# Loading and reducing the last tile of a sum-of-absolute-values kernel in three pieces, with a vector-engine transpose and early stores for the output

## The chip, the cores and the metric

The kernel runs on one core of one Trainium2 chip. The metric is the device time of one execution in microseconds (us), lower is better. The time before is 50.15 us (median of 6 runs, 50.07 to 50.20). The profile covers a span of 48.4 us of this; the remaining 1.75 us lie outside the span and nothing here touches them.

The engines that matter are VectorE (DVE in the profile), ScalarE (ACT), TensorE (PE), and SyncE (SP), which issues most DMAs.

## The reference

```python
batch, dim = 1024, 4096
x = np.random.randn(batch, dim).astype(np.float32)
def reference(x, axis):            # axis = -1
    return np.sum(np.abs(x), axis=axis).astype(np.float32)
```

The input is 16.78 MB and the output 4 KB.

## The kernel before

The 1024 rows are eight tiles of 128 rows. Each tile has a buffer of its own, so no load ever waits for compute. Vector reduces the left 2048 columns of a tile, ACT the right 2048. The ending adds the two halves, transposes the [128 rows, 8 tiles] result on PE so that the store has long rows, copies it out of PSUM (the memory that PE wrote it to) and stores it with one DMA of 8 rows of 512 B.

```python
for t in range(n_tiles):                       # 8
    x_tile = xpool.tile([P, dim], x.dtype)
    nc.sync.dma_start(out=x_tile[:], in_=x[bass.ts(t, P)])
    nc.vector.tensor_reduce(out=vres[:, t : t + 1], in_=x_tile[:, 0:v_cols],
                            axis=X, op=add, apply_absolute_value=True)
    nc.scalar.activation(out=act_scratch[:], in_=x_tile[:, v_cols:dim],
                         func=Abs, accum_out=sres[:, t : t + 1])
res = small.tile([P, n_tiles], fp32)
nc.vector.tensor_add(out=res[:], in0=vres[:], in1=sres[:])
psum_t = psum_pool.tile([P, P], fp32)
nc.tensor.transpose(out=psum_t[0:n_tiles, :], in_=res[:], identity=ident[:])
out_sb = small.tile([n_tiles, P], fp32)
nc.vector.tensor_copy(out=out_sb[:], in_=psum_t[0:n_tiles, :])
nc.sync.dma_start(out=out_tp, in_=out_sb[:])
```

(Enum names are shortened here. Line 53 is the load, 55 the vector reduce, 71 the add, 74 the transpose, 77 the copy, 79 the store.)

## Time and profile before

| what | number | view |
|---|---|---|
| one 2 MB tile arrives every | 4.89 us | timeline: starts of consecutive vector reduces |
| vector reduce of 2048 columns | 2.29 us | groups of instructions |
| ACT on 2048 columns | 1.88 us + 0.19 us accumulator read | groups of instructions |
| last tile landed to end of span | 5.5 us | chain of waits |

First, the rows of the page that cut the span into 40 equal slices: busy tenths of an engine, then the same for the DMA engines, then what they moved.

```profile
DVE  0000000890089007910791069106920692059420
ACT  3600000880078007900690069005900591059100
DMA  0969999999999999999999999999999999300000
GB/s 0 190 217 406 433 433 420 433 433 433 433 433 433 433 433 433 433 433 420 433 433 433 433 433 420 420 420 420 433 433 406 433 433 433 163 0 0 0 3 0
```

The DMA engines are full from slice 4 to slice 34, near 433 GB/s. Vector and ACT are idle more than half the time. So the load stream is the limit, and shortening compute in the middle is worth nothing. The last five slices, about 6 us, have no load in them: there the compute is exposed.

The groups of instructions give the busy time and the mean of one instruction, then the idle time before them and what ended it:

```profile
L55 DVE TENSOR_REDUCE vres<-x_tile 128x1 f32<-128x2048 f32 x8 | 18.3, 2286 | 26.9 <-DMA x_tile<-in_x_dram 26.9
L63 ACT ACTIVATE act_scratch<-x_tile 128x2048 f32<-128x2048 f32 x8 | 15.0, 1881 | 26.9 <-DMA x_tile<-in_x_dram 26.9
```

All idle time of both is waiting for a load. Last, the end of the chain of waits (start in us, duration in us, what):

```profile
4.43 38.41 DMA x_tile<-in_x_dram
42.85 0.02 issue
42.87 2.30 DVE vres L55
...
45.27 0.18 DVE res L71
45.45 0.14 issue
45.58 0.39 PE psum_t L74
45.97 0.02 issue
45.99 0.28 DVE out_sb L77
```

After the last landing at 42.87 come 2.3 us for a whole half tile, 1.1 us from there to the store's issue at 46.30, and 2.1 us from issue to the end at 48.4.

### The profile page before, as it was taken

To read this page: it belongs to the slowest core of one execution; us is meant where nothing else is said; L and a number is where in the kernel's file an instruction comes from. 1 tells how busy PE (TensorE), PEld (TensorE's weight loads), DVE (VectorE), ACT (ScalarE), POOL (GpSimd) and SP (SyncE) were. 2 spreads that over 40 slices of the span, in tenths; PEclk is the share of its full clock that TensorE was granted. 3 is DMA by queue.
4 is the path that set the end of the run, shared out by engine and by line. 5 is a ranking of instruction groups with operands and counts; after the bars stand their busy time and mean duration, and the time that the engine had idled before them with its cause. 6 is when DMAs were issued, how large, how long until landed. Compare 5 with 4: busy or idle time off the path is not lost.

```text
span 48.4 us, 99 instructions
## 1 busy us (share of the span) xinstructions
PE 0.4 (1%) x1; PEld 0.1 (0%) x1; DVE 18.7 (39%) x10; ACT 17.3 (36%) x17; POOL 0.7 (1%) x6
## 2 busy tenths in 40 slices
PE   0000000000000000000000000000000000000300
PEld 0000000000000000000000000000000000000000
DVE  0000000890089007910791069106920692059420
ACT  3600000880078007900690069005900591059100
POOL 5000000000000000000000000000000000000000
DMA  0969999999999999999999999999999999300000
GB/s 0 190 217 406 433 433 420 433 433 433 433 433 433 433 433 433 433 433 420 433 433 433 433 433 420 420 420 420 433 433 406 433 433 433 163 0 0 0 3 0
DMA packets 1168, 16.78 MB, mean 347 GB/s; under 512 B 136, under 2 KB 144, under 8 KB 144
## 3 DMA queue, kind: packets, MB, share of 16 engines
q1 hardware_dynamic: 1168, 16.78, 82.9%
HBM read 16.78 MB, written 0.00 MB: 347 GB/s over the span
## 4 chain that ended last, share of the span: by engine, by line
DMA 79%; SPq 7%; DVE 6%; issue 1%; PE 1%; DVEq 0%
DMA x_tile<-in_x_dram 79%; SPq L53 7%; DVE vres L55 5%; PE psum_t L74 1%; DVE out_sb L77 1%; DVE res L71 0%; DVEq L71 0%
## 5 line engine op out<-in xcount | busy, mean ns | idle before, releaser
L55 DVE TENSOR_REDUCE vres<-x_tile 128x1 f32<-128x2048 f32 x8 | 18.3, 2286 | 26.9 <-DMA x_tile<-in_x_dram 26.9
L63 ACT ACTIVATE act_scratch<-x_tile 128x2048 f32<-128x2048 f32 x8 | 15.0, 1881 | 26.9 <-DMA x_tile<-in_x_dram 26.9
L63 ACT ACT_TABLE_LOAD x1 | 1.3, 1283 | 0.7 <-PEq L96 0.7
L63 ACT ACTIVATION_READ_ACCUMULATOR act_scratch<-x_tile 128x1 f32 x8 | 1.5, 186 | 0.0
L74 PE MATMUL psum_t<-ident,res 128*8 128x128 f32 x1 | 0.4, 372 | 45.6 <-DVE res L71 45.6
L77 DVE COPY out_sb<-psum_t 8x128 f32<-8x128 f32 x1 | 0.3, 279 | 0.6 <-PE psum_t L74 0.6
masks.py:199 POOL TENSOR_SCALAR_AFFINE_SELECT ident<-ident 128x128 f32<-128x128 f32 x1 | 0.3, 292 | 0.1
masks.py:197 POOL MEMSET ident<- 128x128 f32 x1 | 0.2, 205 | 0.3 <-POOLq L96 0.3
L71 DVE TENSOR_TENSOR res<-vres,sres 128x8 f32<-128x8 f32 x1 | 0.2, 166 | 0.1
L74 PEld LDWEIGHTS psum_t<-ident,res 128*8 128x8 f32 x1 | 0.1, 84 | 45.5 <-issue 45.5
L96 POOL MEMSET const-float32-0.0<- 128x1 f32 x1 | 0.1, 98 | 0.2 <-issue 0.2
L96 POOL MEMSET const-bfloat16-1.0<- 128x1 bf16 x1 | 0.1, 101 | 0.0
L96 POOL MEMSET const-uint8-127<- 128x1 uint8 x1 | 0.1, 101 | 0.0
L96 POOL MEMSET const-float32-1.0<- 128x1 f32 x1 | 0.1, 98 | 0.0
## 6 DMA issues: line engine op xcount, KB each, us to landing
x_tile<-in_x_dram SPq DMA_DIRECT2D x8, 2048.0 KB, 25.3
out_dram<-out_sb SPq DMA_DIRECT2D x1, 4.0 KB
```

The source lines that it names most:

```text
L53: nc.sync.dma_start(out=x_tile[:], in_=x[bass.ts(t, P)])
L55: nc.vector.tensor_reduce(out=vres[:, t : t + 1], in_=x_tile[:, 0:v_cols], axis=mybir.AxisListType.X, op=mybir.AluOpType.add, apply_absolu ...
L63: nc.scalar.activation(out=act_scratch[:], in_=x_tile[:, v_cols:dim], func=mybir.ActivationFunctionType.Abs, accum_out=sres[:, t : t + 1],)
L71: nc.vector.tensor_add(out=res[:], in0=vres[:], in1=sres[:])
L74: nc.tensor.transpose(out=psum_t[0:n_tiles, :], in_=res[:], identity=ident[:])
L77: nc.vector.tensor_copy(out=out_sb[:], in_=psum_t[0:n_tiles, :])
L96: nc = _bacc.Bacc("TRN2", target_bir_lowering=False, num_devices=1)
```

## The change

It shortens what lies behind the last landing. It loads the last tile in three DMAs of 2432, 1216 and 448 columns and reduces each as it lands; it finishes and stores the results of the first seven tiles (rows 0 to 6 of the output, seen as 8 rows of 128) while the last one is still loading; and it replaces add, PE transpose and PSUM copy by one small reduce and a vector transpose of 32x32 blocks. Since blocks are transposed in place, the last tile's results (row 7 of the output) for its rows 0 to 31 land in one partition, for rows 32 to 63 in another 32 partitions on, and so forth. By writing the result into columns 0 and 31 of the pad (a tile of 32 columns of zeros that the transpose reads), two of the four land in adjacent partitions (31, 32 and 95, 96), so two stores of two rows suffice, one on SP and one on ACT.

```diff
+LAST_TILE_PIECES = [      # share of columns, share of these to vector
+    (0.59375, 0.50),       # 2432 columns: vector 1216, ACT 1216
+    (0.296875, 0.345),     # 1216 columns: vector 416, ACT 800
+    (0.109375, 1.00),      #  448 columns: vector 448
+]
 ... loads of tiles 0 to 6 as before ...
+    for s, e, _ in pieces:
+        nc.sync.dma_start(out=x_last[:, s:e], in_=last_rows[:, s:e])
 ... reduces of tiles 0 to 6 as before ...
+    nc.vector.tensor_add(out=res06_pad[:, 0:n_full], in0=p06_v[...], in1=p06_s[...])
+    nc.vector.transpose(out=t06[:], in_=res06_pad[:])
+    for b in range(n_blk):                                   # 4 early stores
+        nc.sync.dma_start(out=out_tp[0:n_full, b * BS : (b + 1) * BS],
+                          in_=t06[b * BS : b * BS + n_full, 0:BS])
+    for s, e, ve in pieces:
+        ... vector reduce of [s:ve] and ACT of [ve:e], each into its column of p7 ...
-    nc.vector.tensor_add(out=res[:], in0=vres[:], in1=sres[:])
-    nc.tensor.transpose(out=psum_t[0:n_tiles, :], in_=res[:], identity=ident[:])
-    nc.vector.tensor_copy(out=out_sb[:], in_=psum_t[0:n_tiles, :])
-    nc.sync.dma_start(out=out_tp, in_=out_sb[:])
+    nc.vector.tensor_reduce(out=res7_pad[:, 0:BS:BS - 1],
+        in_=p7[:, 0:n_parts].unsqueeze(1).to_broadcast([P, 2, n_parts]), axis=X, op=add)
+    nc.vector.transpose(out=res7T[:], in_=res7_pad[:])
+    nc.sync.dma_start(out=out7_dram[0:2], in_=res7T[BS - 1 : BS + 1, 0:BS])
+    nc.scalar.dma_start(out=out7_dram[2:4], in_=res7T[3 * BS - 1 : 3 * BS + 1, 0:BS])
```

(Cut and joined where marked; the memsets of the pads and the removal of the identity matrix are left out.)

More of the change, by code (lines that the diff above doesn't have):

```diff
@@ L7, with _round32 @@
 from concourse._compat import with_exitstack
-from concourse.masks import make_identity
-VECTOR_COLS_FRACTION = 0.5
-ACT_SCRATCH_SPACE = "psum"
+VECTOR_FRACTION = 0.5
+LAST_TILE_PIECES = [
[3 more added lines that the diff above has]
+]
+_VEC_NS_PER_COL, _VEC_FIXED = 1.042, 150.0
+_ACT_NS_PER_COL, _ACT_FIXED = 0.833, 480.0
+def _round32(v: int) -> int:
+    return (v // 32) * 32
 @with_exitstack
@@ L24 @@
     P = nc.NUM_PARTITIONS
+    fp32 = mybir.dt.float32
+    BS = nc.vector.STREAM_SQUARE_SIZE
     batch, dim = x.shape
@@ L28 @@
     n_tiles = batch // P
-    v_cols = int(dim * VECTOR_COLS_FRACTION) // 32 * 32
-    v_cols = max(32, min(v_cols, dim))
-    s_cols = dim - v_cols
+    n_full = n_tiles - 1
+    assert n_tiles <= BS, "output transpose layout assumes at most 32 row tiles"
+    assert dim % BS == 0, f"dim {dim} must be a multiple of {BS}"
+    assert P % BS == 0
+    n_blk = P // BS
+    v_cols = _round32(int(dim * VECTOR_FRACTION))
+    v_cols = min(max(v_cols, BS), dim)
+    pieces = []
+    pos = 0
+    for i, (frac, vshare) in enumerate(LAST_TILE_PIECES):
+        if i == len(LAST_TILE_PIECES) - 1:
+            end = dim
+        else:
+            end = min(dim, pos + max(BS, _round32(int(dim * frac))))
+        if end <= pos:
+            continue
+        vec_end = pos + _round32(int((end - pos) * vshare))
+        vec_end = min(max(vec_end, pos), end)
+        pieces.append((pos, end, vec_end))
+        pos = end
+        if pos >= dim:
+            break
+    n_parts = sum((1 if ve > s else 0) + (1 if e > ve else 0) for s, e, ve in pieces)
     out_tp = out.rearrange("(t p) -> t p", p=P)
@@ L38 @@
     psum_pool = ctx.enter_context(tc.tile_pool(name="psum", bufs=1, space=bass.MemoryType.PSUM))
-    ident = small.tile([P, P], mybir.dt.float32)
-    make_identity(nc, ident)
-    vres = small.tile([P, n_tiles], mybir.dt.float32)
-    sres = small.tile([P, n_tiles], mybir.dt.float32)
-    if ACT_SCRATCH_SPACE == "psum":
-        act_scratch = psum_pool.tile([P, s_cols], mybir.dt.float32)
-    else:
-        act_scratch = small.tile([P, s_cols], mybir.dt.float32)
-    for t in range(n_tiles):
-        x_tile = xpool.tile([P, dim], x.dtype)
-        nc.sync.dma_start(out=x_tile[:], in_=x[bass.ts(t, P)])
+    p06_v = small.tile([P, max(n_full, 1)], fp32)
+    p06_s = small.tile([P, max(n_full, 1)], fp32)
+    p7 = small.tile([P, max(n_parts, 1)], fp32)
+    res06_pad = small.tile([P, BS], fp32)
+    nc.gpsimd.memset(res06_pad[:], 0.0)
+    res7_pad = small.tile([P, BS], fp32)
+    nc.gpsimd.memset(res7_pad[:], 0.0)
+    s_max = max(
+        [dim - v_cols] + [max(e - ve, BS) for s, e, ve in pieces]
+    )
+    act_scratch = psum_pool.tile([P, s_max], fp32)
+    x_tiles = []
+    for t in range(n_full):
+        x_tile = xpool.tile([P, dim], x.dtype, name="x_tile")
+        nc.sync.dma_start(out=x_tile[:], in_=x[bass.ts(t, P)])
+        x_tiles.append(x_tile)
+    x_last = xpool.tile([P, dim], x.dtype, name="x_tile")
+    last_rows = x[bass.ts(n_full, P)]
+    for s, e, _ in pieces:
+        nc.sync.dma_start(out=x_last[:, s:e], in_=last_rows[:, s:e])
+    for t in range(n_full):
+        x_tile = x_tiles[t]
         nc.vector.tensor_reduce(
-            out=vres[:, t : t + 1],
+            out=p06_v[:, t : t + 1],
             in_=x_tile[:, 0:v_cols],
@@ L63 @@
         nc.scalar.activation(
-            out=act_scratch[:],
+            out=act_scratch[:, 0 : dim - v_cols],
             in_=x_tile[:, v_cols:dim],
             func=mybir.ActivationFunctionType.Abs,
-            accum_out=sres[:, t : t + 1],
+            accum_out=p06_s[:, t : t + 1],
         )
-    res = small.tile([P, n_tiles], mybir.dt.float32)
-    nc.vector.tensor_add(out=res[:], in0=vres[:], in1=sres[:])
-    psum_t = psum_pool.tile([P, P], mybir.dt.float32)
-    nc.tensor.transpose(out=psum_t[0:n_tiles, :], in_=res[:], identity=ident[:])
-    out_sb = small.tile([n_tiles, P], mybir.dt.float32)
-    nc.vector.tensor_copy(out=out_sb[:], in_=psum_t[0:n_tiles, :])
-    nc.sync.dma_start(out=out_tp, in_=out_sb[:])
+    if n_full > 0:
+        nc.vector.tensor_add(
+            out=res06_pad[:, 0:n_full], in0=p06_v[:, 0:n_full], in1=p06_s[:, 0:n_full]
+        )
+        t06 = small.tile([P, BS], fp32)
+        nc.vector.transpose(out=t06[:], in_=res06_pad[:])
+        for b in range(n_blk):
+            nc.sync.dma_start(
+                out=out_tp[0:n_full, b * BS : (b + 1) * BS],
+                in_=t06[b * BS : b * BS + n_full, 0:BS],
+            )
+    col = 0
+    for s, e, ve in pieces:
+        if ve > s:
+            nc.vector.tensor_reduce(
+                out=p7[:, col : col + 1],
+                in_=x_last[:, s:ve],
+                axis=mybir.AxisListType.X,
+                op=mybir.AluOpType.add,
+                apply_absolute_value=True,
+            )
+            col += 1
+        if e > ve:
+            nc.scalar.activation(
+                out=act_scratch[:, 0 : e - ve],
+                in_=x_last[:, ve:e],
+                func=mybir.ActivationFunctionType.Abs,
+                accum_out=p7[:, col : col + 1],
+            )
+            col += 1
+    nc.vector.tensor_reduce(
+        out=res7_pad[:, 0:BS:BS - 1],
+        in_=p7[:, 0:n_parts].unsqueeze(1).to_broadcast([P, 2, n_parts]),
+        axis=mybir.AxisListType.X,
+        op=mybir.AluOpType.add,
+    )
+    res7T = small.tile([P, BS], fp32)
+    nc.vector.transpose(out=res7T[:], in_=res7_pad[:])
+    out7_dram = out_tp[n_full].rearrange("(b j) -> b j", j=BS)
+    nc.sync.dma_start(out=out7_dram[0:2], in_=res7T[BS - 1 : BS + 1, 0:BS])
+    nc.scalar.dma_start(out=out7_dram[2:4], in_=res7T[3 * BS - 1 : 3 * BS + 1, 0:BS])
 _INS = ['x', 'axis']
```

## The prediction

> **What bounds the kernel now.** The load stream. The page shows the DMA engines at 90% or more and about 430 GB/s from 4 us to 41 us; in the timeline the vector reduces of consecutive 2 MB tiles start 4.89 us apart and last 2.29 us, so compute hides behind loading. Only the ends are exposed. The chain of waits after the last landing: vector reduce of 2048 columns 42.87 to 45.17, add 45.27 to 45.45, PE transpose 45.58 to 45.97, PSUM copy 45.99 to 46.27, output DMA issued 46.30 (0.35 us), end of span 48.4. That is 5.5 us after the last tile landed: 3.4 us of compute, 2.1 us from issue to end. The measured time is 1.75 us above the span.
>
> **What the change does.** It does not touch the 16.8 MB of loads. (1) The last tile comes in pieces of 2432, 1216 and 448 columns, so what must be computed after the last landing shrinks. (2) Rows 0 to 6 are added, transposed and stored before that. (3) Add, PE transpose and PSUM copy become one small vector reduce and one 32x32-block vector transpose; the last store is two 2-row DMAs, on SP and ACT.
>
> **Costs.** Fitting the trace, a vector reduce costs about 0.15 us + 1.04 ns per column (2.286 us at 2048), an ACT piece about 0.18 us + 0.83 ns per column plus a 0.19 us accumulator read. Scaling the 4.89 us per tile from tile 6's landing (37.99), the pieces land near 40.9, 42.35 and 42.9; smaller rows (9.7, 4.9, 1.8 KB instead of 16 KB) may cost 0.1 us more, so 43.0. Vector: 1216 columns to 42.35, 416 to about 43.0, 448 (0.62 us) to about 43.65. ACT: 1216 and 800 columns, finished near 43.4, not last. Rows 0 to 6's add and transpose fit at 40.3 to 40.8, in a hole. Final reduce (estimate 0.18 us, from the 0.17 us add) and transpose (estimate 0.2 us) end near 44.2. The last DMA issues near 44.25 instead of 46.30: 2.05 us earlier. About 1.55 us comes from the shorter last piece, 0.6 us from the shorter tail, less 0.1 us for loading.
>
> **Given back.** Store rows fall from 512 B to 128 B; the Trainium skill, "DMA: Bandwidth & Descriptors", Specifications, puts line rate at 512 B and up, with read-modify-write below. This trace does not show its latency. With six stores to wait for, and an ACT issue, I allow 0.1 us. The last issue to end should stay 2.1 to 2.4 us.
>
> **Predicted:** 48.2 us (span 46.4), 8 in 10 between 47.7 and 49.0. Faster by over 2%: 0.88; within 2%: 0.11; slower: 0.01.
>
> **What would show it right.** Vector's last big reduce has 448 columns, starts at 42.9 to 43.1, and lasts 0.6 us; the last DMA issues at 44.1 to 44.4; DMA slices up to 41 us unchanged; PE idle.
>
> **What would make it wrong.** The four early stores serialising on each other or getting in front of the last loads; false waits between vector and ACT, which write neighbouring columns of one partial-sums tile; SP stalling because ten loads and the stores reuse completion semaphores (the 9th DMA waited 3.7 us for the first load, harmlessly early); short stores with much longer completion; a last piece whose rows land late because one engine lags (in the trace the 16 engines' last packets end from 41.6 to 42.4 us).

## The result, and the profile after

The changed kernel takes 48.04 us (median of 8 runs, 47.94 to 48.09) against 50.09 us (16 runs). The ratio is 0.9585, 95% interval 0.9573 to 0.9598: faster. Ratios here are the mean time of one kernel's fast runs over that of the other's of the same rounds, so they are not quite the ratio of the medians quoted.

The same slices of the page after:

```profile
DVE  0000000594039601980089006930495019889810
ACT  3700000591029400960089005910393019558500
DMA  0959999999999998999999999999999899993000
```

The loads fill the same part of the span; behind them there are now three and a half slices instead of five and a half. A slice is 1.16 us here. The end of the chain of waits after:

```profile
8.58 33.81 DMA x_tile<-in_x_dram
42.40 0.02 issue
42.42 1.16 DVE p L130 x2
43.57 0.03 issue
43.60 0.05 DVEq L147
43.65 0.05 issue
43.70 0.18 DVE res_pad L147
43.88 0.02 issue
43.90 0.21 DVE res7T L154
```

The chain leaves the loads at 42.42, with the landing of the second piece. From there the view follows vector through the reduces of pieces two and three in one go, as there is no gap between them. That does not mean that the third piece was early. Each DMA raises a completion semaphore, a counter, when its data has landed. In the trace's records the third piece's semaphore got its last increment at 42.920, and the reduce of that piece started 0.022 us later, as the second piece's did (42.396 and 42.418). In all eight profiles that reduce these pieces as they land, the third reduce started 0.02 us after that increment:

```profile
42.42 0.59 DVE L130 TENSOR_REDUCE p<-x_tile 128x1 f32<-128x416 f32 x1
42.94 0.62 DVE L130 TENSOR_REDUCE p<-x_tile 128x1 f32<-128x448 f32 x1
```

The two reduces start 0.52 us apart; where all data had landed before (a run below), they start 0.49 us apart. So vector waited some 0.03 us for the third piece (0.02 to 0.06 us in the other seven): landing and compute end almost together, and the landing last. The timeline of the ending (start, duration, engine, line, operation) shows both engines:

```profile
40.39 0.17 DVE L116 TENSOR_TENSOR res_pad<-p_v,p_s 128x7 f32<-128x7 f32 x1
40.59 0.21 DVE L120 STREAM_TRANSPOSE t<-res_pad 128x32 f32<-128x32 f32 x1
40.83 1.38 SPq L122 DMA_DIRECT2D out_dram<-t  x4
40.90 2.67 DVE L130 TENSOR_REDUCE p<-x_tile 128x1 f32<-128x1216 f32 x3
...
42.48 0.84 ACT L139 ACTIVATE act_scratch<-x_tile 128x800 f32<-128x800 f32 x1 [0.21 <-DMA x_tile<-in_x_dram]
43.25 0.19 ACT L139 ACTIVATION_READ_ACCUMULATOR act_scratch<-x_tile 128x1 f32 x1
43.70 0.17 DVE L147 TENSOR_REDUCE res_pad<-p 128x2 f32<-128x10 f32 x1
43.90 0.21 DVE L154 STREAM_TRANSPOSE res7T<-res_pad 128x32 f32<-128x32 f32 x1
44.14 0.24 SPq L156 DMA_DIRECT2D out_dram<-res7T  x1
44.14 0.57 ACTq L157 DMA_DIRECT2D out_dram<-res7T  x1
```

Rows 0 to 6 are finished in the hole at 40.4 to 40.8, and their four stores are issued until 42.2 while the loads go on. From 40.9 to 43.6 both engines are nearly full; ACT is done at 43.44, vector at 43.56. The stores are issued at 44.14 instead of 46.30.

### The profile page after: what moved, and what is told of

It reads as the page before. It is cut to its first block, busy times and chain, and to the rows that moved or that the text cites. A ratio compares the mean times of both kernels' runs of the same rounds, so it can differ in the third digit from the quotient of the medians.

```text
span 46.3 us, 109 instructions
## 1 busy us (share of the span) xinstructions
DVE 19.3 (42%) x14; ACT 17.6 (38%) x19; POOL 0.4 (1%) x6
## 4 chain that ended last, share of the span: by engine, by line
DMA 90%; DVE 3%; issue 0%; DVEq 0%
DMA x_tile<-in_x_dram 90%; DVE p L130 2%; DVE res7T L154 0%; DVE res_pad L147 0%; DVEq L147 0%
## 5 line engine op out<-in xcount | busy, mean ns | idle before, releaser
L101 DVE TENSOR_REDUCE p_v<-x_tile 128x1 f32<-128x2048 f32 x7 | 16.0, 2286 | 24.2 <-DMA x_tile<-in_x_dram 24.2
L108 ACT ACTIVATE act_scratch<-x_tile 128x2048 f32<-128x2048 f32 x7 | 13.2, 1881 | 24.0 <-DMA x_tile<-in_x_dram 24.0
L130 DVE TENSOR_REDUCE p<-x_tile 128x1 f32<-128x1216 f32 (+2 forms) x3 | 2.6, 876 | 0.2
L139 ACT ACTIVATE act_scratch<-x_tile 128x1216 f32<-128x1216 f32 (+1 forms) x2 | 2.0, 1015 | 1.1 <-DMA x_tile<-in_x_dram 1.1
```

What stands on the lines that cost most here:

```text
L101: nc.vector.tensor_reduce(out=p06_v[:, t : t + 1], in_=x_tile[:, 0:v_cols], axis=mybir.AxisListType.X, op=mybir.AluOpType.add, apply_absol ...
L108: nc.scalar.activation(out=act_scratch[:, 0 : dim - v_cols], in_=x_tile[:, v_cols:dim], func=mybir.ActivationFunctionType.Abs, accum_out=p ...
L130: nc.vector.tensor_reduce(out=p7[:, col : col + 1], in_=x_last[:, s:ve], axis=mybir.AxisListType.X, op=mybir.AluOpType.add, apply_absolute ...
L139: nc.scalar.activation(out=act_scratch[:, 0 : e - ve], in_=x_last[:, ve:e], func=mybir.ActivationFunctionType.Abs, accum_out=p7[:, col : c ...
```

## The experiments

**How they are compared.** Landing times of the loads differ by a few tenths of a us from one execution to the next, for the same code: tile 6 landed between 37.61 and 38.15 us in the profiled runs. So I also measure each profiled run from the landing of tile 6 (the start of its vector reduce), which no run changes except the last one below. The table is worked out from start and end records of the traces, in us: A is tile 6's landing to the issue of the first final store (for the run with early stores taken out, of the first of all stores), B is that issue to the end of the span.

```
run                            A      B     A+B    ratio to before (95% interval)
before                        8.31   2.10  10.41   1
changed kernel                6.18   2.13   8.31   0.9585 (0.9573 to 0.9598)
e5_change_again               6.20   2.14   8.34   0.9594 (0.9567 to 0.9622)
e1_pieces_only                6.74   2.25   8.99   0.9735 (0.9706 to 0.9764)
e2_tail_only                  7.75   2.25  10.00   0.9926 (0.9911 to 0.9941)
e3_no_early_stores            6.15   2.85   9.00   0.9740 (0.9724 to 0.9756)
e4_loads_in_pieces            7.92   2.14  10.06   0.9915 (0.9899 to 0.9932)
e6_one_store                  6.18   2.51   8.69   0.9673 (0.9650 to 0.9697)
e7_both_on_sp                 6.18   2.19   8.37   0.9607 (0.9580 to 0.9635)
e8_tail_two_more_stores       7.73   2.12   9.85   0.9915 (0.9883 to 0.9948)
e9_compute_in_pieces          7.91   2.25  10.16   0.9939 (0.9922 to 0.9955)
e10_one_store_adjacent_rows   6.18   2.01   8.19   0.9562 (0.9537 to 0.9587), wrong on purpose
e11_scalar_store_first        6.19   2.13   8.32   0.9578 (0.9562 to 0.9594)
e12_fused_end                 6.52   2.14   8.66   0.9544 (0.9517 to 0.9571)
```

Theory: the gain is two separate savings behind the last landing, a shorter last reduce and a shorter ending. Rivals: nearly all comes from one of them; or splitting the reduce pays, rather than landing earlier.

### The pieces alone

```diff
 changed kernel, but with the old ending:
-    res06_pad, res7_pad, early transpose, 4 early stores, vector transpose, 2 stores
+    small reduce into res[:, 7:8]; PE transpose; PSUM copy; one store of 8 rows on SP
```

> The last tile loaded and reduced in the same three pieces, but the old ending: final small reduce into column 7, PE transpose, PSUM copy, one 8-row store, no early store. My theory (the gain is two separate savings after the last landing, about 1.6 us from the shorter last piece and 0.5 us from the shorter ending): vector's last 448-column reduce ends near 43.6, the store issues near 44.7 (43.6 plus the old ending's 1.13 us), time 48.5 to 48.6, ratio to before about 0.969. Rival (the ending is what mattered, because PE and PSUM are slow to wake, and pieces only move work): 49.5 or more.

Measured: 48.65 us, ratio 0.9735. The last big reduce started 4.99 us after tile 6's landing, as in the changed kernel (4.98), and A fell by 1.57 us. The store was issued at 44.89, or 44.70 with tile 6's landing moved to the 37.96 of the changed kernel. A is as my theory has it; the time is 0.05 us above its range, and B rose by 0.14 us, which I had not foreseen.

```profile
43.87 0.16 DVE L139 TENSOR_REDUCE res<-p 128x1 f32<-128x5 f32 x1
...
44.17 0.37 PE L146 MATMUL psum_t<-ident,res 128*8 128x128 f32 x1 [44.17 <-DVE res L139]
44.58 0.28 DVE L148 COPY out_sb<-psum_t 8x128 f32<-8x128 f32 x1 [0.56 <-PE psum_t L146]
44.89 0.35 SPq L149 DMA_DIRECT2D out_dram<-out_sb  x1
```

Compare the lines 43.70 to 44.14 of the changed kernel: the old ending takes 1.02 us from the start of the small reduce to the store's issue, the new one 0.44 us.

### The ending alone

```diff
-LAST_TILE_PIECES = [(0.59375, 0.50), (0.296875, 0.345), (0.109375, 1.00)]
+LAST_TILE_PIECES = [(1.0, 0.5)]
```

> The new ending and early stores, but the last tile as one load and two halves of 2048 columns. My theory: vector's last big reduce ends at 45.17 as before, small reduce and block transpose follow, stores issue near 45.75 instead of 46.30, time 49.5 to 49.6, ratio about 0.989. Rival (the ending carries most of the gain): 48.5 or less.

Measured: 49.65 us, ratio 0.9926.

```profile
45.55 0.24 SPq L152 DMA_DIRECT2D out_dram<-res7T  x1
```

Tile 6 landed at 37.81 here. A fell by 0.56 us as expected, but the time by only 0.4 us, just above the range I gave, because B rose by 0.15 us here too.

At the store's issue the two savings add up: 1.57 + 0.56 = 2.13 us, against 2.13 us (8.31 - 6.18) for both together. In time they do not: 1.42 + 0.41 = 1.83 us of A+B against 2.10. The missing 0.27 us is in B, and the next section finds it. Both rivals that give one part nearly all of the gain fall.

### The order in which the end checks its semaphores

The trace's records of SP's semaphore instructions at the end (start to end in us, semaphores waited for; worked out from the records of each trace):

```
before            46.89-47.55 [108],[100]   47.59 [109],[103]    then end at 48.40
changed kernel    45.40-45.42 [108],[103]   45.46 [109],[102]    then end at 46.27
e1_pieces_only    45.35-46.16 [106],[104]   46.20  46.26  46.32  then end at 47.14
e2_tail_only      46.81-46.84 [106],[101]   46.87  46.94  47.00  then end at 47.81
```

Eight completion semaphores serve all DMAs in turn, and at the end SP checks them in a fixed order, about 0.065 us for each instruction. In every row the first entry is the check that the last store held up. Before, and in the changed kernel, one check follows it: 9 and 16 DMAs are issued, so the last store signals semaphore 100 or 108. With 11 or 14 DMAs it signals 104 or 106, and three checks follow: 2 x 0.065 = 0.13 us more. To test this I changed only the number of DMAs of the ending-alone run:

```diff
 e2_tail_only, early stores of blocks 0 and 1 split in rows 0:4 and 4:7 (16 DMAs, not 14)
+            for r0, r1 in ((0, 4), (4, n_full)) if b < 2 else ((0, n_full),):
```

> The run with the new ending and the last tile whole, with two of the early stores split in two, so that 16 DMAs are issued instead of 14. Only this moves: the last two stores then signal the last two of the eight completion semaphores. At the end SP checks semaphores in a fixed order, about 0.065 us for each check; in the run with 14 DMAs four checks came after the one that waited for the last store, and store issue to end was 2.26 us instead of 2.13. My theory: with 16 DMAs one check is left, issue to end 2.12 to 2.16 us, time 0.13 us under that run, ratio to before 0.989 to 0.991 instead of 0.9926. Rival (the 0.13 us was a chance of that profile, or comes from the stores themselves): issue to end 2.2 us or more and ratio unchanged, 0.992 to 0.994, or worse from two more stores.

B was 2.12 us, at the edge of the expected range and inside it: two more DMAs made the end 0.13 us shorter. The other profiles fit: with 14 DMAs and three checks after the last store B is 2.25 us again in a run below (only the reduces in pieces), with 16 DMAs it is 2.13 or 2.14 us in the other five that issue the two final stores on SP and ACT. (The expectation says that four checks followed in the run with 14 DMAs; the records show three.) The time does not resolve it: 49.64 us with runs from 49.33 to 49.80 on a noisier chip, ratio 0.9915 with an interval that holds both theories. So the mechanism is shown in the trace, and what it is worth in time is not.

With this, additivity is restored: 1.83 + 2 x 0.13 = 2.09 us, against 2.10.

### Early stores taken out

```diff
-    4 early stores of rows 0 to 6; 2 final stores of row 7
+    one pad with 8 columns, one transpose, 4 final stores of 8 rows of 128 B (2 on SP, 2 on ACT)
```

> The changed kernel, but rows 0 to 6 are stored at the end together with row 7: the add stays early, one block transpose, four stores of 8 rows of 128 B, two on SP and two on ACT. If the early stores save what they seem to (issue time of two more stores per queue), the end moves by the second issue on each queue: 0.25 to 0.6 us later, 48.3 to 48.6. If early storing is worth nothing, because the stores overlap: within 0.1 us of the changed kernel, 48.0 to 48.15. If early stores cost something by running beside the last loads: faster than 48.0.

Measured: 48.72 us, ratio 0.9740, later than I expected of any theory. A is unchanged, B is 2.85 us instead of 2.13.

```profile
43.83 0.21 DVE L144 STREAM_TRANSPOSE res7T<-res_pad 128x32 f32<-128x32 f32 x1
44.07 0.71 SPq L147 DMA_DIRECT2D out_dram<-res7T  x2
44.07 0.90 ACTq L147 DMA_DIRECT2D out_dram<-res7T  x2
```

The second store on ACT began at 44.68, and its data had moved 1.45 us after the first issue, where in the changed kernel the last data had moved after 0.84 us. That is 0.61 us; the rest is the check order again (the last stores signal 106 and 107, and three checks follow 106). So early storing matters to this ending: with a vector transpose each 32-row block needs a store of its own, and the early stores take those issues off the end. Their data moved from 41.8 to 42.8 us in the changed kernel, behind the loads of the same engines. The fear that they get in front of the loads is not borne out: the last piece's completion came 4.98 us after tile 6's with them, and 4.99 us in this run and in the run of the pieces alone, which have none.

### Only the loads in pieces

```diff
 ending alone, but the last tile loaded in the three pieces; reduced in two halves:
+    vector: x_last[:, 2048:4096] (needs the last piece);  ACT: x_last[:, 0:2048]
```

> The cost of short rows in the load by itself: last tile loaded in three pieces, but reduced in two whole halves, with the vector half the one that needs the last piece, so its start is the last landing. Ending as in the changed kernel. Compared with the run that has the new ending and one whole load. If short rows cost the 0.1 us I allowed, the vector half starts near 42.97 instead of 42.87 and the time is 0.1 us over that run's. If they cost nothing: the same start within 0.03 us and the same time.

Vector's half started 5.06 us after tile 6's reduce, against 4.88 us in the kernel before, and A is 0.17 us more than in the ending-alone run. Not all of that is the load. The last piece's completion signal came 5.00 us after tile 6's; the other 0.06 us passed between the signal and the start of the reduce (0.08 us, where it is 0.02 us in the other runs), since this reduce needs three loads and vector's queue had a separate semaphore instruction before it. By the signals, the last landing came 4.98 to 5.00 us after tile 6's in all nine profiles with these three pieces, and 4.88 to 4.89 us in the four that load the last tile whole. So the shorter rows cost 0.1 us, as I had allowed. The time, 49.63 us, is that of the ending-alone run within the interval, and A+B is only 0.06 us more, because this run issues 16 DMAs and so has the better check order (B is 2.14 instead of 2.25). In the changed kernel the 0.1 us is paid too: vector took up both later pieces on their landing, and the second was about as late as the third (4.46 us after tile 6, against 4.36 us for its 3648 columns at 4.89 us per 4096, an estimate).

### Only the reduces in pieces

```diff
-    for s, e, _ in pieces:
-        nc.sync.dma_start(out=x_last[:, s:e], in_=last_rows[:, s:e])
+    nc.sync.dma_start(out=x_last[:], in_=last_rows)
```

> The changed kernel with the last tile in one load, but still reduced in the same three pieces. If it is the earlier landing that pays (my theory), the pieces only add fixed costs: all reduces start after the last landing, vector ends about 2.5 us after it (1216, 416 and 448 columns: 1.36 + 0.52 + 0.62), store issue about 0.25 us later than with two whole halves, time near 49.8, ratio 0.994 to 0.998. If splitting the reduces between the engines were what pays: 48.5 or less.

Measured: 49.82 us, ratio 0.9939, as the theory of the earlier landing has it.

```profile
42.80 2.44 DVE L129 TENSOR_REDUCE p<-x_tile 128x1 f32<-128x1216 f32 x3 [2.05 <-DMA x_tile<-in_x_dram]
44.14 0.57 DVE L129 TENSOR_REDUCE p<-x_tile 128x1 f32<-128x416 f32 x1
44.63 0.61 DVE L129 TENSOR_REDUCE p<-x_tile 128x1 f32<-128x448 f32 x1
```

(The first line is all three reduces, the others are two of them.) All three start after the one landing and take 2.44 us for 2080 columns, where one reduce of 2048 took 2.29 us. A is 0.16 us more than with two whole halves, less than the 0.25 us I expected. The pieces pay only because most of the columns have landed earlier.

### Two final stores or one

The control was the changed kernel itself.

> The changed kernel as it is, as the control for the runs beside it on the same chip: ratio to before 0.957 to 0.960. In its trace the final SP store to the end of the span takes 2.13 us.

It took 48.00 us (47.81 to 48.14), ratio 0.9594, B 2.14 us: as expected.

```diff
-    nc.sync.dma_start(out=out7_dram[0:2], in_=res7T[BS - 1 : BS + 1, 0:BS])
-    nc.scalar.dma_start(out=out7_dram[2:4], in_=res7T[3 * BS - 1 : 3 * BS + 1, 0:BS])
+    nc.sync.dma_start(out=out7_dram, in_=res7T[0:P:BS, 0:BS])   # result in column 0 only
```

> The changed kernel with one final store on SP of four partitions 32 apart, instead of two stores on SP and ACT. In the changed kernel's trace the SP store's data moved at 44.86 and the ACT store's at 44.96, and the end waited for the later. My theory: one SP store is faster by that 0.1 us, 47.9 to 48.0 if the control is at 48.04. Rival (two queues were chosen because one store of four rows takes longer to issue and to spread): 0.05 to 0.2 us slower than the control.

My expectation was wrong, and the loss is larger than the rival had it: 48.40 us against 48.00, with intervals that do not touch. The issue took 0.60 us, and the data moved 1.23 us after its start, against 0.24 and 0.72 us for the SP store of two adjacent rows. To see whether the distance or the number of rows did it, I stored four adjacent partitions, of which three hold zeros: a wrong result.

```diff
-    nc.sync.dma_start(out=out7_dram, in_=res7T[0:P:BS, 0:BS])
+    nc.sync.dma_start(out=out7_dram, in_=res7T[0:4, 0:BS])       # wrong on purpose
```

> Wrong result on purpose (it stores four adjacent partitions, of which three hold zeros): the single final SP store of four rows again, from four adjacent partitions instead of four partitions 32 apart. The store of rows 32 apart took 0.60 us to issue, with its data 1.24 us after the start of the issue, against 0.24 and 0.72 us for two adjacent rows. If the distance of the rows is the cause: issue of 0.25 to 0.35 us, data 0.75 to 0.85 us after its start, time 47.95 to 48.1. If it is the number of rows or one DMA feeding four engines: issue near 0.6 us, time near 48.4.

The issue lines of the two, rows 32 apart and adjacent:

```profile
44.05 0.60 SPq L156 DMA_DIRECT2D out_dram<-res7T  x1
```

```profile
44.11 0.25 SPq L156 DMA_DIRECT2D out_dram<-res7T  x1
```

The data of the adjacent rows began to move 0.73 us after the start of the issue, B was 2.01 us and the time 47.90 us. So the distance of the partitions costs the time, not the number of rows. (Only steps of 1 and 32 partitions were run; both runs issue 15 DMAs, so the check order is the same.) The change's use of columns 0 and 31 to get pairs of adjacent partitions is what avoids it. Why distant partitions are slower to issue, no run shows.

```diff
-    nc.scalar.dma_start(out=out7_dram[2:4], ...)
+    nc.sync.dma_start(out=out7_dram[2:4], ...)
```

> The changed kernel with the ACT store moved to SP, behind the first. If the two queues save the second issue: the second store issues about 0.3 us after the first and its data moves near 45.15 instead of 44.96, so 0.15 to 0.3 us slower than the control. If issue overlaps: no difference within 0.05 us.

Measured: 48.11 us, ratio 0.9607. Its interval overlaps the control's, so the time does not tell them apart. In the trace the second store's data moved at 45.18, 1.02 us after the first issue, where the ACT store's came 0.82 us after it; but B is only 0.05 us longer than the control's, because the second store signals the semaphore that is checked last. That lies between my two expectations. The second queue is worth 0.05 us of B here, and the 0.11 us between the medians is not resolved. The Trainium skill, "DMA: Bandwidth & Descriptors", section "Issuing engines are not separate DMA queues", says that issuing from several engines saves only the sequencer's issue time; this trace agrees, and shows how little that is when the issue is 0.24 us.

### Two attempts to go further

```diff
-    nc.sync.dma_start(out=out7_dram[0:2], ...); nc.scalar.dma_start(out=out7_dram[2:4], ...)
+    nc.scalar.dma_start(out=out7_dram[2:4], ...); nc.sync.dma_start(out=out7_dram[0:2], ...)
```

> The changed kernel with the two final stores in the other program order, so that the slower ACT store should get the completion semaphore that is checked last. My theory (a check after the blocking one costs 0.065 us): from the issue of the stores to the end 2.06 to 2.08 us instead of 2.13, time 0.05 to 0.07 us under the changed kernel, which the interval may not resolve. Rival: issue to end unchanged at 2.12 to 2.14.

The edit did not do what it was meant to: the semaphores came out as before, 109 for SP and 108 for ACT. B is 2.13 us and the time 47.99 us, as for the changed kernel. It tests nothing of the theory.

```diff
 last tile: pieces of 2048, 1024, 608 and 416 columns (to vector: 800, 640, 448, 416)
+    x_last has n_parts - 1 more columns, which hold the partial sums of the earlier pieces
+    last reduce: in_=x_last[:, s : ve + n_parts - 1], out=res7 (one column, the total)
+    nc.vector.transpose(out=res7T[:], in_=res7[:].to_broadcast([P, BS]))
-    small reduce over p7
 tiles 0 and 1 in one load (16 DMAs again); ACT store first
```

> An attempt to beat the changed kernel: last tile in four pieces (2048, 1024, 608, 416 columns); the earlier partial sums lie behind the last piece's columns, so the last vector reduce of 422 columns gives the total and the small final reduce goes; the transpose reads that one column broadcast; ACT store first; the first two tiles in one load, so that 16 DMAs are issued and the last stores signal the last semaphores. From tile 6's landing to the store issue 5.9 us instead of 6.18, issue to end 2.07 instead of 2.13 us: 0.25 to 0.35 us under the changed kernel, 47.65 to 47.8, ratio 0.952 to 0.955. If vector and ACT miss the planned times (the last reduce must wait for ACT's last partial sum), the gain shrinks to nothing: 48.0.

The result is correct. Six runs gave 47.68, 47.69, 47.69, 47.92, 48.02 and 48.06 us, ratio 0.9544 (0.9517 to 0.9571). Three of them are where I expected them and three are no better than the changed kernel. The profiled run is one of the longer three:

```profile
42.62 0.31 ACT L137 ACTIVATE act_scratch<-x_last 128x160 f32<-128x160 f32 x1
42.86 0.18 ACT L137 ACTIVATION_READ_ACCUMULATOR act_scratch<-x_last 128x1 f32 x1
43.27 0.59 DVE L128 TENSOR_REDUCE res<-x_last 128x1 f32<-128x422 f32 x1
43.89 0.21 DVE L146 STREAM_TRANSPOSE res7T<-res 128x32 f32<-128x32 f32 x1
```

The idea works: the transpose follows the last big reduce directly. But that reduce started at 43.27, 5.65 us after tile 6's landing, though ACT was done at 43.04 and the fourth piece had landed by 43.07. It reads the partial sum of vector's third reduce, which ended at 43.18, and that one had started on its landing: the loads were late. The second piece landed 4.20 us after tile 6, where the stream's pace gives about 3.7 us for its 3072 columns (an estimate from 4.89 us per 4096), and the last load packet ended 5.13 us after tile 6's landing, where in the changed kernel it was 4.46. Whether the fourth piece, the double first load or chance made them late is open. The interval still touches that of the control, which ran in another call, so I do not call this version faster than the changed kernel. With the ACT store first B is 2.14 us here too, not the 2.07 I expected.

## Why the prediction was right

I predicted 48.2 us, between 47.7 and 49.0; the time is 48.04. Point by point:

- *"Only the ends are exposed."* Right. Up to tile 6's landing the loads take the same time in both profiles (37.99 and 37.96), and all of the gain lies behind tile 6's landing: A+B fell by 2.10 us, the time by 2.05.
- *"About 1.55 us comes from the shorter last piece, 0.6 us from the shorter tail."* Measured alone: 1.57 and 0.56 us at the store's issue, 2.13 us together, where the prediction came to 2.05. Its 1.55 us is 45.17 less 43.62 (a landing at 43.0 and a reduce of 0.62 us), which already holds the 0.1 us for loading, as the measured 1.57 does; the list of terms takes that 0.1 us off a second time.
- *"Vector's last big reduce has 448 columns, starts at 42.9 to 43.1, and lasts 0.6 us; the last DMA issues at 44.1 to 44.4."* It started at 42.94 and lasted 0.62 us; the stores were issued at 44.14.
- *"Final reduce (estimate 0.18 us ...) and transpose (estimate 0.2 us)."* 0.17 and 0.21 us.
- *"Fitting the trace, a vector reduce costs about 0.15 us + 1.04 ns per column."* The trace before has one width only, 2048 columns, which cannot give both constants; they stand in the changed kernel's source (150 ns and 1.042 ns). The widths after bear them out: 1.42, 0.59 and 0.62 us for 1216, 416 and 448 columns, against 1.41, 0.58 and 0.62 us.
- *"less 0.1 us for loading"*: Right in size, though counted twice in the sum. The last landing came 4.98 us after tile 6's instead of 4.88, and the third reduce started on it, so the third piece's landing was on the critical path as predicted, though only 0.03 us behind vector's own work.
- *"I allow 0.1 us"* for short stores. B rose by 0.03 us. Of the 0.16 us between 48.2 and 48.04, 0.11 us is the issue of the stores, at 44.14 instead of 44.25; most of the rest is rounding (a span of 46.4 and 1.75 us make 48.15).
- *What would make it wrong.* None came about: the early stores did not hold up the loads, vector and ACT did not wait for each other inside the pieces, and no reused semaphore delayed anything that mattered.
- *What it lacked.* It gave the early stores no value of their own, since it took the short ending as a whole. Taking them out costs 0.7 us, of which 0.13 is the check order. And it did not see that the number of DMAs sets how many checks follow the last store; the changed kernel happens to issue 16, which is as good as the 9 of before. That part of the hit was luck: with 14 DMAs B would have been some 0.13 us longer, by the runs above.

## What to carry to other kernels

When a stream of loads is the limit, look at what lies behind the last landing: cut the last load so that each piece's compute fits into the time that the next piece takes to land, and stop when the engines are busy throughout, for then smaller pieces add only fixed costs (here 0.15 us for two more reduces and 0.1 us for the loads). Move every result that does not need the last load, and its store, in front of it. When two savings do not add up in time, compare them at an event in the middle of the chain, such as the last store's issue; the difference may lie behind it. And where a chain of waits runs through an engine without a gap, compare the landing times as well: an engine that seems busy throughout may have been released by a landing each time.

## What the Trainium skill lacked or had wrong

- "DMA: Bandwidth & Descriptors" has no cost for a store from SBUF partitions that are far apart. Four rows of 128 B from partitions 32 apart took 0.60 us to issue on SP, with the data 1.23 us after the start of the issue; from adjacent partitions 0.25 and 0.73 us.
- "DMA: Bandwidth & Descriptors", Specifications, puts read-modify-write below 512 B. At the end of this kernel no cost of it shows, in a comparison of different stores: from the start of the issue to the last completion signal the 8 rows of 512 B (one store) took 1.23 us, the 2 + 2 rows of 128 B (two stores) 1.24 us.
- "Perfetto Trace Analysis", Summary: the profiler window per engine type, says that the window of a DMA instruction hides the data movement. The trace agrees, and adds a trap: the same two-row store lasts 0.57 us on ACT and 0.24 us on SP, but its data moved only 0.10 us later. Both were issued at the same moment in every run, so whether ACT is slower or waited for SP's issue is open.
- No page says that the completion semaphores are checked one after the other in a fixed order at the end of such a kernel, or what the last store's place in that order is worth: about 0.065 us for each check that follows, 0.13 us between three checks and one.
